# The merged projection's row blocks: the next block's turn moved between two output halves, and a buffer moved between two state tags

## The chip, the cores and the metric

The kernel runs on one core of one Trainium2 chip. The metric is the device time of one execution in microseconds (us). The notation of the profile is: PE is TensorE (PEld its weight loads), DVE is VectorE, ACT is ScalarE, POOL is GpSimd, SP is the engine that issues most of the transfers. L1227 is line 1227 of the kernel.

## The reference, cut to what matters

One layer of a diffusion backbone works on 9 blocks of 128 rows: block 0 is the prompt (128 tokens), blocks 1 to 8 are the 1024 latent tokens. Attention heads and four bidirectional mLSTM heads stand side by side and are merged by one output projection, which a SwiGLU feed-forward layer follows.

```python
attn_o = attention(aq, keys, vals)
hm, st_f, st_b = mlstm_bidir(heads(mq), heads(mk) * (MLSTM_DK ** -0.5), heads(mv), gates, init_f, init_b)
hm = rmsnorm(hm.transpose(0, 2, 1, 3), mlstm_norm_w.reshape(MLSTM_HEADS, MLSTM_DV))
hm = (hm.reshape(B, T, MLSTM_WIDTH) * jax.nn.sigmoid(mo.astype(F32))).astype(x.dtype)
mix = jnp.concatenate([attn_o, hm], axis=-1) @ w_out
x = x + g1 * mix
h2 = rmsnorm(x, norm2_w) * (1 + sc2) + sh2
x = x + g2 * swiglu(h2, w_gu, w_down)
```

The mLSTM scan carries a matrix state of 128x128 and a vector of 128 for each head and direction. The latent tokens' scans start from states that are given as inputs, `state_C` and `state_n`.

## The kernel before, in words

A product in fp32 is made of three matmuls: each operand is split into a high part (a cast on ACT) and the rest (a subtraction, mostly on DVE), and the products high·high, high·low and low·high are added in PSUM. So a weight piece needs a transfer, a cast (L157, `whi`) and a subtraction (L137, `wlo`), and a block of rows needs to be turned by PE (L116, four transposes of 128x128), cast on ACT and subtracted on DVE before it can be multiplied.

The program has three long stretches.

*The mLSTM heads.* For head h, `head_project` makes q, k, v and gate products of all 9 blocks and adds each block to the states: the forward state at once (L824, DVE), while the backward contributions are put aside by ACT (L828, tag `cs`). `head_mlstm` then runs the backward chain over blocks 8 to 2 (L862, DVE, seven steps) and the scan over blocks 0 to 8; it is woven with the projection of the next head and with the first third of the attention. Each head loads two initial states (L807 and L808 on SP's queue): `c0f` for the forward scan, `c0b` for the backward one. The backward one is read by the first step of L862 and for the last time by the matmul L898 at block 8, the last block of the scan. `c0f` has two buffers, `c0b` one; the running states have `CSB` = 21 buffers of the tag `cs`, and each head takes 16 of them.

*The prefill* (`prefill`, L1188). It computes the mLSTM half of the merged projection for all 9 blocks. `load_hm` brings a block's normalised mLSTM rows from DRAM (tag `hmr`, two buffers), `mix(b)` turns them (L116) into one PSUM bank, casts them (L1227, ACT) and subtracts (L137, DVE) into a tile of the tag `mx` (three buffers, one of which holds the prompt's gate `gx_all` at first). `half(b, n)` multiplies them with one of two halves of the output columns: 12 matmuls (L1183 to L1185) into one bank, then DVE multiplies by the gate (L1144, or L1243 for blocks 6 to 8) and POOL adds it to the row (L1145 or L1244). The pool of such banks has four. `end(b)` makes the sum of squares for blocks 0 to 2 (L1345, ACT, which needs POOL's additions of both halves), and after blocks 2, 3 and 4 the second norm of rows 0, 1 and 2 (`norm2`: L1361, eight transposes, L1371, L1376). After every yield of the prefill 0.35 of a step of the second third of the attention is woven in (S at L1075, maximum L1077, exponential L1078, L1081, L1082, transposing transfers L1084 and L1085, values L1099 and L1100), and each of its PE steps is held behind the last output matmul written so far.

*The feed-forward stretch*, for three groups of three blocks: `gate_up` (L1382 to L1384) and `down` (L1155 to L1157), with the rest of the attention woven in.

What sets the order: a planner goes through the program with a model of each instruction's time and, on each engine, takes the ready instruction with the highest priority. Priority is the order in which the code is written, except that a `hot(n)` block counts as written n instructions earlier. The order that comes out is fixed; on the chip each engine works it off in turn, and an instruction that waits holds all behind it on its engine. Buffers are given out of a pool for each tag, and an instruction that needs one waits until one is released.

Of the kernel before, what the change touches and what calls it, by code (L numbers as in the profile page):

```python
# [8 lines left out]
F32 = mybir.dt.float32  # L9
# [10 lines left out]
P = 128  # L20
D = 1024
KD = D // P
NB = 9
# [14 lines left out]
LAST = [(0, 5), (5, 5), (10, 4), (14, 4), (18, 4)]  # L38
PAIRS = [(0, 1), (2, 3), (4,), (5, 6), (7, 8)]
NG = 4  # L40
CSB = 21
SINGLES = [(b,) for b in range(NB)]


# [1 line left out]
def hybrid_step(ctx: ExitStack, tc: tile.TileContext, I: dict, O: dict):  # L46
# [8 lines left out]
    def hot(n):  # L55
        return tc.high_priority(n)

    def nm(s):
        uid[0] += 1
        return f"{s}_{uid[0]}"  # L60
# [19 lines left out]
    def xrow(b):  # L80
        if b == 0:
            return I["x_prompt"][0]
        return I["x_sample"][0, (b - 1) * P : b * P, :]
# [20 lines left out]
    def bank():  # L104
        return psum["mm"].tile([P, 512], F32, name=nm("mm"), tag="mm")
# [9 lines left out]
    def transpose(out, in_, n=P):  # L115
        nc.tensor.transpose(out, in_, ident[:n, :n])  # L116
# [19 lines left out]
    def sub(out, full, hi, eng):  # L136
        (dve if eng == "dve" else pool).tensor_tensor(out=out, in0=full, in1=hi, op=ALU.subtract)  # L137
# [410 lines left out]
    mlp = es1.enter_context(tc.tile_pool(name="mlp", bufs=1, reuse_waits="tile"))  # L548
    mwh = mlp.tile([P, 512], F32, name="mwh")
    for tag, shape, bufs, dt in (("hm", [P, NB, P], 2, F32), ("ssh", [P, NB], 2, F32), ("nu", [P, 2, P + 1], 4, F32), ("it", [P, 2, P + 1], 3, F32),  # L550
                                 ("dn", [P, 2], 3, F32), ("jkh", [P, P], 1, BF16), ("sd", [P, 2, P], 4, F32), ("dt", [P, 2, P], 4, F32),
                                 ("so", [P, P], 9, F32), ("va", [P, P + 1], 9, F32), ("kT", [P, P], 9, F32), ("th", [P, P], 1, F32),
                                 ("kt", [P, P], 2, F32), ("wv", [P, 2, P + 1], 2, F32), ("c0f", [P, P + 1], 2, F32), ("c0b", [P, P + 1], 1, F32),
                                 ("cs", [P, P + 1], CSB, F32), ("qTm", [P, CT], 2 * NCH, F32)):
        mlp.tile(shape, dt, name=f"lay_{tag}", tag=tag, bufs=bufs)

# [2 lines left out]
    def gate_work(mlp):  # L559
        def g1(name, dt=F32, rows=P):  # L560
            return mlp.tile([P, P + 1], dt, name=name, tag="cs", bufs=CSB)[0:rows, 0:P]

# [211 lines left out]
    def head_project(h, st):  # L774
# [28 lines left out]
        st["s"] = states = {}  # L803
        st["raw"] = raws = {}
        for d in range(2):
            c0 = mlp.tile([P, P + 1], F32, name=nm("c0"), tag=("c0f", "c0b")[d], bufs=2 - d)
            dma(c0[:, 0:P], I["state_C"][0, 0, d, h])  # L807
            dma(c0[:, P : P + 1], I["state_n"][0, 0, d, h].rearrange("(p o) -> p o", o=1))  # L808
            states[d, 1 if d == 0 else NBL] = c0

        def update(b, kt, va):
# [6 lines left out]
            for d in range(2):  # L818
                if b == (NBL if d == 0 else 1):
                    continue  # L820
                add = pc[:, d * (P + 1) : (d + 1) * (P + 1)]
                cn = mlp.tile([P, P + 1], F32, name=nm("cs"), tag="cs", bufs=CSB)
                if d == 0 and b > 0:
# [314 lines left out]
    def t2():  # L1138
        return ft.tile([P, 512], F32, name=nm("t2"), tag="t2", bufs=3)

    def add_gated(x1, ps, g, n, eng=dve):
        cs = slice(n * 512, (n + 1) * 512)
        t = t2()
        dve.tensor_tensor(out=t, in0=ps, in1=g, op=ALU.mult)  # L1144
        eng.tensor_tensor(out=x1[:, cs], in0=x1[:, cs], in1=t, op=ALU.add)  # L1145
# [17 lines left out]
    def out_pieces(half, n):  # L1163
        pieces = []
        for j in range(2):
            r0 = half * 512 + 2 * j * P
            rows = w_out[r0 : r0 + 2 * P, n * 512 : (n + 1) * 512].rearrange("(a p) n -> p a n", p=P)
            pieces.append(load_piece([(full_view, rows)], (2, 512)))
        return pieces

    def out_gates():
        gs = []
        for n in range(2):
            gl = xg.tile([P, 512], F32, name=nm("gl"), tag=("gl", "gx")[n], bufs=1)
            dma(gl, g_d[0, 1:2, n * 512 : (n + 1) * 512].to_broadcast([P, 512]))
            gs.append(gl)
        return gs

    def out_block(ws, n, th, tl):
        ps = bank()  # L1180
        for k in range(4):
            wh, wl = ws[n][k // 2]
            mm(ps, th[:, k], wh[:, k % 2, :], start=(k == 0), stop=False)  # L1183
            mm(ps, th[:, k], wl[:, k % 2, :], start=False, stop=False)  # L1184
            loaded["pe"] = mm(ps, tl[:, k], wh[:, k % 2, :], start=False, stop=(k == 3)).ins  # L1185
        return ps

    def prefill(cur, nxt):  # L1188

        x1s = cur["x1"], nxt["x1"]  # L1190
        cur["rs"] = []

        def load_hm(b):
            if b >= NB:
                return None
            hm = xe.tile([P, 512], F32, name=nm("hmr"), tag="hmr", bufs=2)
            if b < CB:
                loaded["hm"] = dma(hm, hm_d[0][b * P : (b + 1) * P, :]).ins
            else:
                r = dma(hm.rearrange("p (h n) -> p h n", n=P), hm_d[b // CB][:, :, b % CB * P : (b % CB + 1) * P])  # L1200
                if b == CB:
                    loaded["hm"] = r.ins
            return hm

        def load_x1(b):
            if CB <= b < 2 * CB:
                dma(x1s[1][b % CB], xrow(b))

        hms = [load_hm(0), load_hm(1)]
        ws = [out_pieces(1, 0)]  # L1210
        gs = out_gates()
        gx_all = xe.tile([P, D], F32, name="gx_all", tag="mx", bufs=3)
        gate = loaded["gate"] = dma(gx_all, g_d[0, 0:1, :].to_broadcast([P, D])).ins
        ws.append(out_pieces(1, 1))
        cur["gate"] = loaded["piece"]
        gx = [gx_all[:, n * 512 : (n + 1) * 512] for n in range(2)]
        mixed = {}

        def mix(b):
            t = xe.tile([P, NQ, P], F32R, name=nm("mx"), tag="mx", bufs=3)  # L1220
            th, tl = mixed[b] = t[:, 0:4], t[:, 4:8]
            hm = hms.pop(0)
            ps = bank()
            for j in range(4):
                transpose(ps[:, j * P : (j + 1) * P], hm[:, j * P : (j + 1) * P])
            psv = ps.rearrange("p (j x) -> p j x", j=4)
            nc.scalar.copy(th, psv)  # L1227
            sub(tl, psv, th.bitcast(F32), "dve")
            with tc.issue_after(gate):
                hms.append(load_hm(b + 2))  # L1230

        def half(b, n):
            c, i = divmod(b, CB)
            cs = slice(n * 512, (n + 1) * 512)
            ps = out_block(ws, n, *mixed[b])
            g = gx[n] if b == 0 else gs[n]
            if c < 2:
                add_gated(x1s[c][i], ps, g, n, pool)
            else:
                xt = t2()  # L1240
                dma(xt, xrow(b)[:, cs])
                t = t2()
                dve.tensor_tensor(out=t, in0=ps, in1=g, op=ALU.mult)  # L1243
                pool.tensor_tensor(out=xt, in0=xt, in1=t, op=ALU.add)  # L1244
                dma(x1_d[i][:, cs], xt)

        def end(b):
            if b < CB:
                with hot(200):
                    cur["rs"] += stats(x1s[0][b : b + 1])  # L1250
            if 2 <= b < CB + 2:
                yield from norm2(0, cur, b - 2)

        for b in range(2):
            mix(b)
            yield
        for b in range(2):
            half(b, 0)
            yield
        for b in range(2):  # L1260
            load_x1(b + 2)
            half(b, 1)
            yield
            yield from end(b)
        for b in range(2, NB):
            load_x1(b + 2)
            mix(b)
            yield
            for n in range(2):
                half(b, n)  # L1270
                yield
            yield from end(b)

    def attn_out_first(oT, ready):
# [66 lines left out]
    def stats(rows):  # L1341
        s1 = fp.tile([P, CB], F32, name=nm("s1"), tag="s1", bufs=3)
        for i, x in enumerate(rows):
            jk = ft.tile([P, D], BF16, name=nm("jk"), tag="t2", bufs=3)
            act(jk, x, AF.Square, accum_out=s1[:, i : i + 1])  # L1345
        r = rsqrt(fp, s1[:, 0 : len(rows)], len(rows), 1.0 / D, CB)
        return [r[:, i : i + 1] for i in range(len(rows))]
# [174 lines left out]
    for _ in prefill(cur, nxt):  # L1522
        due += 0.35
        while due >= 1.0:
            with tc.issue_after(cur["gate"]), tc.issue_after(loaded["gate"]), tc.issue_after(loaded["hm"]), tc.issue_after(loaded["pe"]):
                next(att, None)
            due -= 1.0
# [100 lines left out]
```

## Time and profile before

| | us |
|---|---|
| median of three runs | 1536.48 (1536.39 to 1541.33) |
| the profiled execution | 1540.57 |
| its span, first to last instruction | 1538.8 |
| PE busy in the span | 1479.7 |
| DVE, ACT, POOL busy | 1019.1, 771.3, 272.3 |

The prefill's first transposes start at 489.59 us, its last output matmul starts at 576.8 us, and the feed-forward stretch fills the rest. In the views, a row of the timeline gives the start, the duration, the engine, the line, the operation, its tiles and, in brackets, how long the engine stood idle before it and what ended that. A row of stretches gives for each engine the busy time and the number of instructions, then the granted clock of TensorE, the busy share of the transfer engines and their rate. A matmul's duration in the trace includes its way through the array, so that the distance between the starts of two matmuls tells more than their durations.

### The profile page before, as it was taken

Reading aid. Unit: us, or ns where it says so; the run is one execution under the profiler, and the core shown is the slowest. Engines: PE = TensorE matmul, PEld = TensorE weight load, DVE = VectorE, ACT = ScalarE, POOL = GpSimd, SP = SyncE. Lnnn points to the kernel's source line nnn. Section 1 sums busy time; section 2 is a strip of 40 time slices with the busy share of each in tenths; the row PEclk is TensorE's granted clock in tenths of the full one; section 3 lists DMA queues with packets and bytes.
Section 4 is the critical chain, followed back from the end, with each engine's and each line's share of the span. In section 5 each row is a group of like instructions: output and inputs, shape, how many; then the busy total and the mean of one; then the engine's idle time right before and its main releaser. Section 6 shows DMA issues by size and latency. Waiting matters only on the chain.

```text
span 1538.8 us, 23409 instructions
## 1 busy us (share of the span) xinstructions
PE 1479.7 (96%) x8539; PEld 1245.3 (81%) x8539; DVE 1019.1 (66%) x2025; ACT 771.3 (50%) x1429; POOL 272.3 (18%) x354
## 2 busy tenths in 40 slices
PE   6799999999989899999999999999999999999997
PEld 3545567677766679899898989989898989999996
DVE  4878654838657875878646497887856584554554
ACT  4764475847654544555332445556553443333333
POOL 0112423233434441010010101000010101101110
PEclk9799999999999999999999999999999999999998
DMA  9664323523365566978634457877754445544441
GB/s 359 191 203 148 100 71 42 119 52 66 75 212 167 156 145 193 214 152 199 170 123 149 152 154 239 188 175 175 181 135 143 145 155 160 157 131 137 141 142 60
DMA packets 387113, 233.77 MB, mean 152 GB/s; under 512 B 170102, under 2 KB 347462, under 8 KB 386998
## 3 DMA queue, kind: packets, MB, share of 16 engines
q1 hardware_dynamic: 385006, 228.69, 54.0%
q10 hardware_dynamic: 1864, 3.20, 1.1%
q8 instruction: 67, 1.10, 0.3%
q14 instruction: 48, 0.39, 0.1%
q0 software_dynamic: 128, 0.39, 0.1%
HBM read 182.21 MB, written 11.69 MB: 126 GB/s over the span
## 4 chain that ended last, share of the span: by engine, by line
PE 58%; DVE 3%; DMA 1%; ACT 1%; issue 0%; ACTq 0%
PE mm L1383 12%; PE mm L1384 12%; PE mm L1382 12%; PE mm L1155 5%; PE mm L1156 5%; PE mm L1157 5%; PE S L1075 3%; PE po L1099 1%; PE po L1100 1%; PE mm L1185 1%; PE mm L1184 1%; PE mm L1183 1%; DVE fl L1371 1%; DVE wlo L137 1%; DVE t L1144 0%; DVE x L1145 0%
## 5 line engine op out<-in xcount | busy, mean ns | idle before, releaser
L157 ACT CAST whi<-raw 128x1024 fp32r<-128x1024 f32 (+1 forms) x216 | 221.8, 1027 | 390.3 <-PE mm L1383 151.5
L137 DVE TENSOR_TENSOR wlo<-raw,whi 128x1024 fp32r<-128x1024 f32 (+1 forms) x216 | 260.4, 1205 | 183.4 <-ACT whi L157 182.8
L1383 PE MATMUL mm<-aTl,whi 128*128 128x384 f32 x1056 | 355.9, 337 | 2.7 <-DVE aTl L137 2.7
L1384 PE MATMUL mm<-aTh,wlo 128*128 128x384 f32 x1056 | 354.1, 335 | 0.0
L1382 PE MATMUL mm<-aTh,whi 128*128 128x384 f32 x1056 | 352.5, 335 | 0.0
L137 POOL TENSOR_TENSOR hl<-tn,hl 128x384 fp32r<-128x384 f32 x66 | 85.3, 1292 | 848.7 <-ACT hl L1405 713.8
L1383 PEld LDWEIGHTS mm<-aTl,whi 128*128 128x128 f32 x1056 | 198.4, 188 | 3.9 <-DVE aTl L137 3.3
L1384 PEld LDWEIGHTS mm<-aTh,wlo 128*128 128x128 f32 x1056 | 198.4, 188 | 0.1
L1382 PEld LDWEIGHTS mm<-aTh,whi 128*128 128x128 f32 x1056 | 198.0, 188 | 0.6
L1156 PE MATMUL mm<-wlo,hl 128*128 128x512 f32 x372 | 145.3, 391 | 0.0
L1155 PE MATMUL mm<-whi,hl 128*128 128x512 f32 x372 | 144.1, 392 | 0.0
L1157 PE MATMUL mm<-whi,hl 128*128 128x512 f32 x372 | 142.6, 392 | 0.0
L1082 DVE SCALAR_TENSOR_TENSOR pl<-pr,st,ph 128x1152 f16<-128x1152 f32 (+1 forms) x72 | 96.0, 1334 | 33.0 <-ACT ph L1081 32.9
L1078 ACT ACTIVATE pr<-S,st 128x1152 f32<-128x1152 f32 (+1 forms) x72 | 81.2, 1128 | 34.5 <-DVE st L1077 33.9
L1077 DVE TENSOR_REDUCE st<-S 128x1 f32<-128x1152 f32 (+1 forms) x72 | 88.9, 1235 | 13.6 <-PE S L1075 12.9
L1081 ACT ACTIVATE ph<-pr,st 128x1152 f16<-128x1152 f32 (+1 forms) x72 | 83.8, 1164 | 20.9 <-DVE st L1080 8.0
L506 PE MATMUL wi<-headw,hT 128*128 128x384 f16 x288 | 93.9, 326 | 0.2 <-ACT th L792 0.2
L508 PE MATMUL wi<-headw,hT 128*128 128x384 f16 x288 | 93.9, 326 | 0.0
L507 PE MATMUL wi<-headw,hT 128*128 128x384 f16 x288 | 93.9, 326 | 0.0
L1144 DVE TENSOR_TENSOR t<-mm,gl 128x512 f32<-128x512 f32 x102 | 68.8, 685 | 27.5 <-DMA gl<-g_d 12.2
L1075 PE MATMUL S<-kst,qT 128*128 128x384 f32 (+1 forms) x400 | 84.4, 344 | 2.4 <-ACT pr L1078 2.4
L1157 PEld LDWEIGHTS mm<-whi,hl 128*128 128x128 f32 x372 | 69.9, 188 | 14.4
(396 smaller groups left out, 2647.7 us busy)
## 6 DMA issues: line engine op xcount, KB each, us to landing
raw<-in_w_gu_dram SPq DMA_DIRECT2D x132, 512.0 KB
raw<-in_w_down_dram SPq DMA_DIRECT2D x60, 512.0 KB
a<-in_w_ada_dram SPq DMA_DIRECT2D x24, 512.0 KB
gl<-g_d SPq DMA_DIRECT2D x36, 256.0 KB
aw<-in_w_ada_dram SPq DMA_DIRECT2D x16, 512.0 KB
iraw<-in_w_in_dram SPq DMA_DIRECT2D x32, 256.0 KB
raw<-in_w_out_dram SPq DMA_DIRECT2D x12, 512.0 KB
x<-in_x_sample_dram SPq DMA_DIRECT2D x11, 512.0 KB
```

Source lines behind the costliest of these rows:

```text
L137: (dve if eng == "dve" else pool).tensor_tensor(out=out, in0=full, in1=hi, op=ALU.subtract)
L157: nc.scalar.copy(hi[:, :n], raw[:, :n])
L506: mm(ps[:, :n], ah, wh[:, k % 2, c0 : c0 + n], start=(k == 0), stop=False)
L507: mm(ps[:, :n], ah, wl[:, k % 2, c0 : c0 + n], start=False, stop=False)
L1075: mm(S[:, n, 0:w], qT[:, h, :], kst[kv][:, t, c0 + n * w : c0 + (n + 1) * w], start=(t == 0), stop=(t == 1))
L1082: dve.scalar_tensor_tensor(out=plv, in0=prv, scalar=st[:, 3:4], in1=phv, op0=ALU.mult, op1=ALU.subtract)
L1155: mm(ps, ah, wh[:, k % 2, :], start=(k == 0), stop=False)
L1156: mm(ps, ah, wl[:, k % 2, :], start=False, stop=False)
L1157: mm(ps, al, wh[:, k % 2, :], start=False, stop=(k == nk - 1))
L1382: mm(ps, wh[:, k, :], th[:, k, :], start=(k == 0), stop=False)
L1383: mm(ps, wh[:, k, :], tl[:, k, :], start=False, stop=False)
L1384: mm(ps, wl[:, k, :], th[:, k, :], start=False, stop=(k == KD - 1))
```

## The change

In the prefill, `mix(b + 1)` now stands between `half(b, 0)` and `half(b, 1)` for blocks 2 to 7, `mix(2)` stands between `half(0, 1)` and `half(1, 1)`, and the loop no longer begins a block with its own `mix`. `end(0)` comes before `mix(2)`. No instruction is added or removed there. The tag `c0b` gets a second buffer, and the tag `cs` loses one of its 21; a buffer of either has the same size.

```diff
-CSB = 21
+CSB = 20
...
-                                 ("kt", [P, P], 2, F32), ("wv", [P, 2, P + 1], 2, F32), ("c0f", [P, P + 1], 2, F32), ("c0b", [P, P + 1], 1, F32),
+                                 ("kt", [P, P], 2, F32), ("wv", [P, 2, P + 1], 2, F32), ("c0f", [P, P + 1], 2, F32), ("c0b", [P, P + 1], 2, F32),
...
-            c0 = mlp.tile([P, P + 1], F32, name=nm("c0"), tag=("c0f", "c0b")[d], bufs=2 - d)
+            c0 = mlp.tile([P, P + 1], F32, name=nm("c0"), tag=("c0f", "c0b")[d], bufs=2)
...
-        for b in range(2):
-            load_x1(b + 2)
-            half(b, 1)
-            yield
-            yield from end(b)
+        load_x1(2)
+        half(0, 1)
+        yield
+        yield from end(0)
+        load_x1(3)
+        mix(2)
+        yield
+        half(1, 1)
+        yield
+        yield from end(1)
         for b in range(2, NB):
             load_x1(b + 2)
-            mix(b)
-            yield
-            for n in range(2):
-                half(b, n)
+            half(b, 0)
+            yield
+            if b + 1 < NB:
+                mix(b + 1)
                 yield
+            half(b, 1)
+            yield
             yield from end(b)
```

More of the change, by code (lines that the diff above doesn't have):

```diff
@@ L1259, in prefill @@
             yield
-        for b in range(2):
-            load_x1(b + 2)
+        load_x1(2)
[8 more added lines that the diff above has]
+        yield from end(1)
+        for b in range(2, NB):
+            load_x1(b + 2)
+            half(b, 0)
[3 more added lines that the diff above has]
+                yield
             half(b, 1)
             yield
-            yield from end(b)
-        for b in range(2, NB):
-            load_x1(b + 2)
-            mix(b)
-            yield
-            for n in range(2):
-                half(b, n)
-                yield
             yield from end(b)
```

## The prediction

> **What bounds the kernel now.** First the page's busy shares and its forty slices, for the engine that is full and where it is not; then stretches of 25 us around the prefill.
>
> ```profile
> PE 1479.7 (96%) x8539; PEld 1245.3 (81%) x8539; DVE 1019.1 (66%) x2025; ACT 771.3 (50%) x1429; POOL 272.3 (18%) x354
> PE   6799999999989899999999999999999999999997
> PEclk9799999999999999999999999999999999999998
> ...
> 475.00:500.00 25.00, 22.14 (x119) 16.27 (x118) 18.80 (x68) 12.49 (x37) 11.75 (x14) 0.93 0.56 180
> 500.00:525.00 25.00, 21.00 (x88) 15.94 (x87) 21.97 (x60) 15.75 (x25) 9.85 (x6) 0.90 0.65 196
> 525.00:550.00 25.00, 22.46 (x121) 18.76 (x120) 20.00 (x35) 13.41 (x23) 15.31 (x10) 0.96 0.48 102
> 550.00:575.00 25.00, 24.32 (x133) 19.98 (x133) 15.65 (x25) 10.61 (x13) 8.83 (x6) 1.00 0.65 160
> 600.00:1525.00 925.00, 922.32 (x5043) 855.65 (x5042) 609.78 (x870) 411.84 (x542) 84.25 (x65) 1.00 0.59 158
> ```
>
> PE is the bound: from 600 to 1525 us it stands idle for 925 − 922.3 = 2.7 us at full clock, so that stretch gives nothing and only moves forward or back as a whole. The prefill, 489 to 577, is where PE has holes and where the granted clock falls below 1. Who makes the holes is in the waits of PE from 485 to 600.
>
> ```profile
> PE mm L1183 <- ACT mx L1227: 4.8, 4, 2.3
> PE S L1075 <- ACT pr L1078: 1.6, 1, 1.6
> PE mm L1185 <- DVE mx L137: 1.2, 2, 0.9
> PE mm L1185 <- DVE rv L127: 0.3, 1, 0.3
> ```
>
> The output matmuls wait for the cast of the block's own rows (L1227), and then for its subtraction (L137). The fourth row is the same subtraction, in block 2, put down to another DVE instruction that ended last. The change aims at these rows. One of the four casts is block 0's, which the change leaves where it is; the worst is block 3's:
>
> ```profile
> 491.81 0.49 PE L1183 MATMUL mm<-whi,mx 128*128 128x512 f32 x1 [1.13 <-ACT mx L1227]
> ...
> 517.07 0.60 PE L116 MATMUL mm<-ident,hmr 128*128 128x128 f32 x4
> 519.99 0.77 PE L1183 MATMUL mm<-whi,mx 128*128 128x512 f32 x1 [2.32 <-ACT mx L1227]
> 521.50 0.80 PE L1185 MATMUL mm<-whi,mx 128*128 128x512 f32 x1 [0.32 <-DVE mx L137]
> 526.79 0.44 PE L1185 MATMUL mm<-whi,mx 128*128 128x512 f32 x1
> ...
> 512.20 0.39 PE L1183 MATMUL mm<-whi,mx 128*128 128x512 f32 x1
> 512.43 0.39 PE L1184 MATMUL mm<-wlo,mx 128*128 128x512 f32 x1
> ...
> 518.32 1.06 ACT L1345 ACTIVATE jk<-x1a 128x1024 bf16<-128x1024 f32 x1 [3.57 <-POOL x1a L1145]
> 519.37 0.56 ACT L1227 CAST mx<-mm 128x512 fp32r<-128x512 f32 x1
> ...
> 516.00:520.00 4.00, 1.68 (x16) 1.41 (x14) 3.90 (x8) 1.69 (x4) 1.58 (x2) 1.00 0.61 132
> 520.00:524.00 4.00, 3.68 (x8) 2.48 (x9) 3.79 (x21) 4.00 (x7) 0.00 (x0) 0.51 0.08 24
> 524.00:528.00 4.00, 4.00 (x14) 3.12 (x13) 2.10 (x5) 1.23 (x3) 0.98 (x1) 0.64 0.39 74
> ```
>
> Block 3's rows are turned by 517.67, but ACT stands at L1345, block 2's sum of squares, which waits 3.57 us for POOL; the cast is behind it, and PE, with nothing else left, behind the cast. Then the granted clock is 0.51 for four microseconds and 0.64 for the next. The 14 steps between matmul starts from 519.99 to 526.79 take 6.80 us; at the step of the undisturbed rows, 0.23, they would take 3.2. Of the 3.6 lost, 0.32 is the wait for the subtraction, and 3.3 the clock.
>
> **The change part by part.** *The moved turns, what goes.* `mix(2)` to `mix(8)` move: each has four transposes on PE, one cast, one subtraction and the issue of one `hmr` load on SP. None is added. The waits that should end: casts 4.8 − 1.13 (block 0) = 3.7 us; subtractions 1.2 + 0.3 = 1.5; and the clock behind block 3's hole, 3.3, since the rows of 516 to 528 show the fall directly behind the only stretch in which PE did 1.68 of 4 us. That is 8.5 us gross.
>
> *What covers a moved turn.* The path from transposes to subtraction is block 2's:
>
> ```profile
> 507.67 0.60 PE L116 MATMUL mm<-ident,hmr 128*128 128x128 f32 x4
> 508.31 0.58 ACT L1227 CAST mx<-mm 128x512 fp32r<-128x512 f32 x1 [1.77 <-PE mm L116]
> 509.74 0.68 DVE L137 TENSOR_TENSOR mx<-mm,mx 128x512 fp32r<-128x512 f32 x1
> ```
>
> It ends at 510.42, 2.75 us after the first transpose, and PE itself is engaged for about 0.4 of it (eight transposes take 1.03 us in a row below, four 0.60). The cover is `half(b, 1)`: 12 steps of 0.23, 2.8 us, plus whatever attention stands behind it. So the cover is just enough when ACT and DVE come at once. In block 3 the same path took 521.50 − 517.07 = 4.4 us with ACT held up, 1.6 more than the cover; under the change the cast is written ahead of the sum of squares that held it. The new remainder lies between 0 and 1.6 for each of the three blocks that are beside the second norm (4.8); as DVE is busy 21.97 of 25 us there, I take 0.5 each, 1.5 in all.
>
> *Banks.* The turn's bank is now held beside both halves' banks, and the norm takes two of the four as well:
>
> ```profile
> 514.92 0.39 PE L1185 MATMUL mm<-whi,mx 128*128 128x512 f32 x1
> 516.20 1.03 PE L116 MATMUL mm<-ident,y 128*128 128x128 f32 x8
> 516.26 0.68 DVE L1144 TENSOR_TENSOR t<-mm,gl 128x512 f32<-128x512 f32 x1
> 523.24 1.04 DVE L1371 TENSOR_SCALAR fl<-mm,scale,shift 128x128 f32<-128x128 f32 x3
> ```
>
> The norm's eight transposes at 516.20 fill two banks that DVE empties only at 523.24 + 1.04. In that time one half, one turn and the next half have to share two, and a half's bank comes free 516.26 + 0.68 − 514.92 − 0.39 = 1.6 us after its last matmul. So PE may newly wait up to 1.6 us before `half(b, 1)`, less the 0.4 of transposes, in three blocks: 0 to 3.6; I take 1.5, since DVE's queue was the slow part in the rows above too.
>
> *Queues.* On SP each `hmr` load moves forward with its turn; it waits for its buffer, so the transposing transfers of the attention queue behind it. The buffer comes free with the transposes, which PE does without waiting, and block 4's load, after block 2's turn, has the whole of block 3 to land: nothing. POOL gets no instruction earlier or later but by its inputs. On ACT, a cast that waits for an `mx` tile would hold the sums of squares; for block 2 that tile is block 0's, free with the last matmul of `half(0, 1)`, just before: nothing. The wait of S for the exponential (1.6) belongs to the attention and stays; its end is a gain of 1.6.
>
> *The second `c0b`.* Now the last head's load can be issued only after the scan before has read the buffer:
>
> ```profile
> 446.60 0.26 ACT L828 COPY cs<-mm 128x129 f32<-128x129 f32 x1
> 441.58 0.56 SPq L808 DMA_DIRECT2D c<-in_state_n_dram  x1
> 447.86 1.24 DVE L131 TENSOR_TENSOR rt<-ry 128x9 f32<-128x9 f32 x1
> 449.30 0.35 DVE L862 SCALAR_TENSOR_TENSOR cs<-c,decb,cs 128x129 f32<-128x129 f32 x1 [0.20 <-DMA c<-in_state_n_dram]
> 450.04 0.49 PE L875 MATMUL mm<-qT,kT 128*128 128x128 f32 x2 [2.42 <-DVE sd L883]
> 448.00:456.00 8.00, 5.11 (x36) 3.56 (x37) 7.80 (x22) 2.68 (x8) 3.04 (x2) 0.79 0.49 159
> ```
>
> The load takes from 441.58 to 449.3 to land, while the last block's contribution is there at 446.86. But DVE is busy until 449.10 with other work, so the wait itself is 0.20 us. The best case is that the planner, with the state early, draws the chain forward and PE's hole of 8 − 5.11 = 2.9 us and the clock loss of the same row (0.21 × 8 = 1.7) go: 4.6. The worst is that the seven steps of 0.35, 2.4 us, come ahead of the `sd` (L883) that PE waits for. I take a gain of 0.5, by the row of the wait itself.
>
> *One `cs` fewer.* In the third head:
>
> ```profile
> L828 ACT COPY cs<-mm x9: 267/269/318, 322.7 to 376.3; 128x129 f32<-128x129 f32 x9
> L898 PE MATMUL mm<-cs,qT x28: 273/275/276, 309.6 to 366.7; 128*128 128x129 f32 x28
> ```
>
> The scan of the head before has read its states by 366.7, while this head's contributions come in until 376.3. Halfway, at 350, this head holds about 8 of its 16, and the scan, 40 of 57 us through, keeps about 5: 13 of 20. So it costs nothing; were the scan three blocks later, one wait of about a scan's block, 57/7 = 8 us, could appear.
>
> *The sum*: −8.5 + 1.5 + 1.5 − 0.5 = −6.0 us. The profiled execution (1540.57, of which 1538.8 span) is 4.1 above the median; a difference carries over, so from 1536.48 comes **1530.5 us**. Behind the prefill nothing gives it back, because PE is full there.
>
> On the clock, the rows above show a fall after a hole of 2.32 us. The Trainium skill, "TensorE: Matmul & The Clock Gate", Part 1, says that the clock halves after at least one idle window of about 3.4 us. The trace agrees in the factor (0.51) and differs in the length, as PE was idle no 3.4 us on end. By that rule the fall would not be the hole's, the 3.3 would stay, and the time would be 1533.8.
>
> **The rivals.** *A, slower: banks.* The place is `half(b, 1)` in blocks 3, 4 and 5, where two banks are with the norm. If PE's new wait there grows past about 2 us, the clock falls again, and one such wait costs what block 3's costs now: 2.3 + 0.3 + 3.3 = 5.9. Three cost 17.7, against 8.5 saved: 1545.7. It decides from two such waits on. For it: DVE's 88% from 500 to 525. Against it: a half's bank lag of 1.6 less 0.4 is under 2.
>
> *B, it does nothing.* The planner ranks by written order but starts what is ready; if it keeps ACT at the sum of squares ahead of the cast, or the attention's S ahead of the half, the waits only change place: 1536.5, within 2. Against it: the cast is now written one half ahead of that sum.
>
> *C, the clock falls anyway.* A similar hole, 2.42 before 450.04, stands in the row with clock 0.79; the hole of 1.6 before S is followed by nothing like it, as the clock of 525 to 550 is 0.96, and what lacks there is the tail of block 3's fall. If it isn't the hole's length that decides, a window of PE's lesser work elsewhere in the prefill gets the low clock: 1530.5 + 3.3 = 1533.8.
>
> *D, more.* No remainder, no bank waits, the wait of S gone, and the start of the last scan drawn forward: −8.5 − 1.6 − 4.6 = −14.7, 1521.8.
>
> **How the numbers follow.** Forecast (1527 to 1534): 0.38. A: 0.16, B: 0.18, C: 0.13, D: 0.15. 0.5% of the median is 7.7 us, about what a measurement of this kernel tells from no change. Faster than 1528.8: D and a quarter of the forecast's chance, 0.25. Slower than 1544.2: most of A, 0.13. Same: 0.62. The range reaches from near D's end to where A has one and a half of its waits: 1523 to 1541.
>
> **What would show it.** The row of L1183 waiting for L1227 should shrink to block 0's, in about 1.1 us; no L1227 should stand behind an L1345 that waits for POOL; the clock from 500 to 550 should be 1 but for the start at 491.81; the transposes of block b + 1 should stand between two halves on PE; the last prefill matmul should come some 6 us earlier. L807 for the last head's `c0b` should be issued long before 441, with no wait of L862 for it. The prediction is wrong if PE waits for L1144 or L1243 to free a bank, if the clock falls in blocks 3 to 5, or if the heads' stretch ends more than 3 us from where it does.

## The result, and the profile after

| | before | after |
|---|---|---|
| median of 13 runs of each, us | 1540.67 | 1535.38 |
| the profiled execution, us | 1540.57 | 1535.49 |
| its span, us | 1538.8 | 1533.7 |

The ratio is 0.9972, with a 95% interval of 0.9964 to 0.9980: 4.3 us less (3.1 to 5.5; the two medians lie 5.3 apart), where the forecast had 6.0. That is a real gain and a small one, within the 0.5% that the forecast had called no change. The 1530.5 itself lies 4.9 below the median, and 4.2 of that is the base: the three runs of the kernel before that were shown have a median of 1536.48, and the 13 runs here 1540.67. Two executions of kernels in the experiments took 5172.03 and 1663.96 us, and the medians and ratios given there are those of the others.

The first view is the waits of PE from 485 to 600 us in the changed kernel (engine, operation and line, what it waited for, then us in total, times, longest). Below L1257 a line of the changed kernel has a number higher by 7: L1352 is the old L1345, L1368 the old L1361, L1389 the old L1382.

```profile
PE S L1075 <- ACT pr L1078: 3.1, 1, 3.1
PE mm L1184 <- DVE wlo L137: 1.9, 4, 0.6
PE mm L1185 <- DVE mx L137: 1.7, 1, 1.7
PE mm L1183 <- ACT mx L1227: 1.1, 1, 1.1
...
PE mm L1183 <- DVE st L1080: 0.5, 1, 0.5
...
PE mm L1183 <- DVE mx L137: 0.3, 1, 0.3
```

The wait for the cast has shrunk from 4.8 to block 0's 1.1, as forecast. The wait of S for the exponential, which the prediction left at 1.6, is now 3.1 and the largest. The last two rows are waits of a half for a bank, 0.8 us in all; how that is seen stands with the account of the prediction. Next the same stretches as before the change, and four of 4 us around block 3 (length, busy time of each engine, then the granted clock):

```profile
475.00:500.00 25.00, 20.85 (x101) 15.10 (x101) 18.40 (x61) 12.49 (x32) 10.62 (x13) 1.00 0.62 202
500.00:525.00 25.00, 19.64 (x89) 16.14 (x89) 21.67 (x52) 14.11 (x22) 8.84 (x6) 0.93 0.70 192
525.00:550.00 25.00, 24.11 (x133) 20.09 (x132) 21.66 (x44) 14.82 (x26) 14.73 (x11) 1.00 0.42 91
550.00:575.00 25.00, 25.00 (x137) 20.54 (x137) 16.56 (x26) 10.62 (x15) 7.72 (x6) 1.00 0.77 193
...
512.00:516.00 4.00, 2.98 (x15) 2.33 (x13) 4.00 (x12) 1.04 (x3) 2.47 (x1) 1.00 0.75 148
516.00:520.00 4.00, 1.67 (x8) 1.35 (x9) 3.90 (x16) 2.44 (x4) 1.28 (x1) 0.97 0.09 18
520.00:524.00 4.00, 4.00 (x16) 3.48 (x15) 3.76 (x7) 4.00 (x8) 0.00 (x0) 0.61 0.38 72
524.00:528.00 4.00, 4.00 (x21) 3.26 (x20) 3.27 (x10) 4.00 (x7) 1.91 (x2) 1.00 0.61 137
```

From 525 on the prefill is nearly full (24.11 and 25.00 of 25, against 22.46 and 24.32). At block 3 PE is not: it does 1.67 of 4 us, almost the 1.68 of before, and the clock falls behind it. The hole has not gone; other instructions stand around it. The timeline of PE, with one row of DVE and one of ACT:

```profile
513.54 1.21 PE L1075 MATMUL S<-kst,qT 128*128 128x384 f32 x6
514.59 0.40 PE L1185 MATMUL mm<-whi,mx 128*128 128x512 f32 x1
518.12 1.32 PE L1075 MATMUL S<-kst,qT 128*128 128x384 f32 x6 [3.14 <-ACT pr L1078]
...
521.22 0.78 PE L1183 MATMUL mm<-whi,mx 128*128 128x512 f32 x1
...
515.38 1.35 DVE L1077 TENSOR_REDUCE st<-S 128x1 f32<-128x1152 f32 x1
...
516.76 1.22 ACT L1078 ACTIVATE pr<-S,st 128x1152 f32<-128x1152 f32 x1 [3.72 <-DVE st L1077]
```

Between two S of the attention stands one matmul of block 2's second half. S has a single buffer, so the second waits until the exponential of the first has read it: S, maximum on DVE (held 0.6 us by the small steps of a reciprocal root), exponential on ACT, 4.6 us in all. The first half of block 3, whose rows are ready, stands behind the second S and the norm's transposes and begins at 521.22, at half clock.

Two numbers carry the comparisons that follow. The prefill is counted from the first turn to the first gate matmul of the feed-forward stretch, and that stretch from its first gate matmul to the start of its last. In the changed kernel:

```profile
L116 PE MATMUL mm<-ident,hmr x36: 270/272/328, 487.2 to 560.9; 128*128 128x128 f32 x36
...
L1389 PE MATMUL mm<-aTh,whi x1056: 331/334/423, 572.3 to 1505.9; 128*128 128x384 f32 x176
```

So the prefill takes 85.1 us and the stretch 933.6. For all kernels that were profiled, with the granted clock from 508 to 532 us, where block 3 lies:

| kernel (executions) | prefill, us | feed-forward, us | clock 508 to 532 |
|---|---|---|---|
| before (3) | 87.4, 87.2, 87.0 | 934.0, 933.1, 934.3 | 0.86, 0.86, 0.93 |
| buffers alone | 87.4 | 933.1 | 0.93 |
| after (2) | 85.1, 84.6 | 933.6, 933.2 | 0.93, 0.93 |
| turns alone | 83.5 | 934.8 | 0.93 |
| before, attention one step later | 87.9 | 938.1 | 0.93 |
| after, attention one step later | 82.4 | 937.0 | 1.00 |
| after, held up to block 3 (2) | 82.1, 82.9 | 933.3, 934.2 | 1.00, 1.00 |
| after, held to the last steps | 81.5 | 935.1 | 1.00 |

A clock of 0.93 over 24 us is a loss of 0.07 × 24 = 1.7 us, and 0.86 one of 3.4. The clock column leaves out block 0. There the clock of 488 to 498 is 0.83, a loss of 1.7 us, in two of the three executions of before, in one of the two of after and in one of the two held up to block 3, and 1.00 in the others of these. So two prefills of this table can differ by 1.7 us for no reason of an edit.

### The profile page after: what moved, and what is told of

Same layout as the page of the kernel before. It is cut to its first block, busy times and chain, and to the rows that moved or that the text cites. A ratio compares the mean times of both kernels' runs of the same rounds, so it can differ in the third digit from the quotient of the medians.

```text
span 1533.7 us, 23404 instructions
## 1 busy us (share of the span) xinstructions
PE 1475.5 (96%) x8539; PEld 1242.4 (81%) x8539; DVE 1019.8 (66%) x2025; ACT 772.3 (50%) x1429; POOL 266.7 (17%) x354
## 4 chain that ended last, share of the span: by engine, by line
PE 61%; DVE 3%; ACT 1%; issue 0%; DVEq 0%
PE mm L1390 12%; PE mm L1391 12%; PE mm L1389 12%; PE mm L1155 5%; PE mm L1156 5%; PE mm L1157 5%; PE S L1075 3%; PE po L1099 2%; PE po L1100 2%; PE mm L1183 1%; PE mm L1185 1%; PE mm L1184 1%; DVE fl L1378 1%; DVE wlo L137 1%; DVE t L1144 0%; DVE x L1145 0%
## 5 line engine op out<-in xcount | busy, mean ns | idle before, releaser
L137 DVE TENSOR_TENSOR wlo<-raw,whi 128x1024 fp32r<-128x1024 f32 (+1 forms) x216 | 260.4, 1206 | 182.4 <-ACT whi L157 180.8
L1389 PE MATMUL mm<-aTh,whi 128*128 128x384 f32 x1056 | 353.1, 335 | 0.0
L137 POOL TENSOR_TENSOR hl<-tn,hl 128x384 fp32r<-128x384 f32 x66 | 83.8, 1270 | 847.4 <-ACT hl L1412 755.5
L1389 PEld LDWEIGHTS mm<-aTh,whi 128*128 128x128 f32 x1056 | 198.1, 188 | 0.5
L1144 DVE TENSOR_TENSOR t<-mm,gl 128x512 f32<-128x512 f32 x102 | 68.7, 684 | 24.7 <-DMA gl<-g_d 9.3
```

Of the source, the lines that this page charges most:

```text
L1389: mm(ps, wh[:, k, :], th[:, k, :], start=(k == 0), stop=False)
```

## The experiments

**The turns alone.** The changed kernel with the buffers of before.

```diff
-CSB = 20
+CSB = 21
...
-("c0b", [P, P + 1], 2, F32)
+("c0b", [P, P + 1], 1, F32)
...
-tag=("c0f", "c0b")[d], bufs=2)
+tag=("c0f", "c0b")[d], bufs=2 - d)
```

> Edit: the moved turns alone; cs keeps 21 buffers and c0b one. Theory T (the whole gain is the moved turns): ratio to the kernel before 0.997, the same as with the whole change, and the prefill (first turn to first feed-forward matmul) takes about 85 us against 87.4. Rival R1 (the earlier load of the initial state carries part: the first 450 us were 3 us shorter in the changed kernel's profile): ratio 0.9985 to 1.0. Rival R2 (the lost cs buffer costs something that the whole change hides): ratio under 0.996.

Measured: 1534.88 us, ratio 0.9969 (0.9957 to 0.9980), the whole of the change's gain, as theory T has it. In its waits of PE stand the same two rows, the cast's at block 0's size and that of S:

```profile
PE S L1075 <- ACT pr L1078: 3.1, 1, 3.1
...
PE mm L1183 <- ACT mx L1227: 1.1, 1, 1.1
```

**The buffers alone.** The kernel before with the second `c0b` and one `cs` fewer (the lines above, the other way round).

> Edit: the kernel before with cs at 20 and c0b at two buffers, turns not moved. T: ratio 1.000, within 0.0005, since PE, DVE, ACT and POOL keep their order through the heads and the chain's wait for the load was 0.20 us; the prefill has its 2.3 us hole before block 3 and the clock falls there. R1: ratio 0.998 to 0.9985. R2: over 1.0005.

Measured: 1540.13 us, ratio 0.9999 (0.9989 to 1.0010). The buffers are worth nothing that can be measured. What they do is in the changed kernel's DVE timeline: the first step of the last backward chain no longer waits for its state, but PE's wait behind the chain stays (the last row is from the waits of PE from 430 to 600, where it was 2.4).

```profile
446.12 0.34 DVE L862 SCALAR_TENSOR_TENSOR cs<-c,decb,cs 128x129 f32<-128x129 f32 x1
...
451.13 2.09 DVE L862 SCALAR_TENSOR_TENSOR cs<-cs,decb,cs 128x129 f32<-128x129 f32 x1
...
PE mm L875 <- DVE sd L883: 2.1, 1, 2.1
```

From first to last step the chain takes 5.0 us, as before (449.30 in the prediction's row to 454.33). The load was never what it waited for, but for 0.2 us.

**The attention one step later, in both kernels.** If the hole at block 3 is the S that now stands too early, holding all attention phases of the prefill back by one step should take it out.

```diff
-    due = 0.0
+    due = -0.35
     for _ in prefill(cur, nxt):
         due += 0.35
```

> Edit: the changed kernel, with the attention woven into the prefill one yield later (its count starts at -0.35). So the scores of each attention head are written behind a half that is ready, where the changed kernel has them ahead of block 3's first half. Theory T2 (the changed kernel still has block 3's hole in front of a scores matmul that waits 3.1 us for the exponential, and the clock falls behind it for 3.4 us): that wait goes, PE waits in the prefill fall from about 10 us to about 5, a further 3 to 5 us are gained, ratio 0.994 to 0.995. Rival R3 (the attention is the true chain of the prefill, so the wait only changes place, or comes back in the feed-forward stretch where more of the attention is left): ratio 0.997 as before the edit.

> Edit: the kernel before, turns not moved, with the attention one yield later as in e3. T2 with T (the two are separate: the turn's path of 2.75 us stays open in front of every block): casts still hold PE for 3 to 4 us in all, ratio 0.998 to 1.0. Rival R4 (the attention's place is all that matters, and the moved turns are worth nothing of their own): the ratio of e3.

Measured: the changed kernel held back 1537.74, ratio 0.9984 (0.9974 to 0.9993); the kernel before held back 1543.99, ratio 1.0022 (1.0013 to 1.0031). The turns are worth as much in this position of the attention as in the other (0.9984 against 1.0022), but holding back costs both kernels something, and the expected gain on top did not come. Yet the hole did go: S waits 0.6 us instead of 3.1, the clock stays at 1 and the prefill is 2.7 us shorter. The feed-forward stretch is 3.4 us longer, which is the second form of rival R3: theory T2 is right about the hole and wrong about the time. The rows of that stretch, from the timelines of PE, ACT and SP and from the stretches:

```profile
584.81 0.37 PE L1099 MATMUL po<-phT,vs 128*128 128x256 f16 x1 [2.73 <-DMA phT<-ph]
...
577.25 1.22 ACT L1078 ACTIVATE pr<-S,st 128x1152 f32<-128x1152 f32 x1
...
580.32 1.98 SPq L1084 DMA_TRANSPOSE phT<-ph  x1
...
580.00:592.00 12.00, 9.27 (x53) 8.44 (x53) 6.37 (x7) 5.65 (x8) 1.00 (x1) 0.86 0.81 186
```

The first value product of the feed-forward waits 2.73 us for a transposing transfer, and the clock falls behind it: 2.7 + 0.14 × 12 = 4.4 us lost. The chain behind that transfer begins with the last S of the prefill, which ran a step later; its exponential came at 577.25. In the changed kernel that exponential is at 571.57, and nothing waits. In the kernel before, held back, the same product waits 2.4 us, and the waits for the cast grow to 7.5 us, where 3 to 4 were expected, because an S has moved on that stood between turn and half in block 5, for example, and covered the cast:

```profile
PE mm L1183 <- ACT mx L1227: 7.5, 6, 2.3
PE po L1099 <- DMA phT<-ph: 2.4, 1, 2.4
```

**Held back only up to block 3, or to the last steps.** Two kernels keep the later S at block 3 and catch up afterwards, one right behind it and one six steps further on.

```diff
-    due = 0.0
-    for _ in prefill(cur, nxt):
-        due += 0.35
+    due = -0.35
+    for step, _ in enumerate(prefill(cur, nxt)):
+        due += 0.7 if step == 14 else 0.35
```

> The changed kernel with the attention's phases of the prefill held back by one step up to block 3 and caught up right behind it, so that from block 4 on the order is that of the changed kernel. Theory T3 (holding back the attention is worth something at block 3, and what the held-back kernel lost it lost to one transpose by DMA at the first value product of the feed-forward): the wait of S for the exponential shrinks from 3.1 us to under 1, the clock stays at 1 from 508 to 540, and no value product waits for phT behind 575 us. Gain against the changed kernel about 2.5 (wait) + 1.6 (0.13 of 12 us of clock) = 4 us, ratio to the kernel before 0.9945 (0.993 to 0.996). Rival R4 (the value product waits for its transposes again, though the last S stands where the changed kernel has it): as the held-back kernel, 0.998. Rival R5 (the hole at block 3 is filled with an attention phase that was free elsewhere, so that another hole opens by block 6): as the changed kernel, 0.997.

The other has `step == 20`.

> As the kernel that holds back by one step all through, but the attention catches up at the last step but a few, so that only the last S of the prefill stands again where the changed kernel has it (between the two halves of the last block). Theory T3: what decides is how early that last S is issued before the first value product of the feed-forward; the 2.7 us wait for phT and the half clock behind it go, and the time is that of e5, ratio 0.9945 (0.993 to 0.996). Rival R4 (the wait comes from the traffic of the transfers at the start of the feed-forward, or from all phases being late): it stays above 1.5 us and the ratio is 0.997 to 0.999.

Measured: held up to block 3, 1532.22, ratio 0.9955 (0.9942 to 0.9968); held to the last steps, 1534.97, ratio 0.9970 (0.9959 to 0.9980). The first does at block 3 what theory T3 says, and its ratio lies in the range given, but the gain over the changed kernel is about 2.6 us by the ratios and not 4. Its rows at block 3, from the timeline of PE and the stretches:

```profile
512.82 1.22 PE L1075 MATMUL S<-kst,qT 128*128 128x384 f32 x6
...
515.84 0.48 PE L1183 MATMUL mm<-whi,mx 128*128 128x512 f32 x1
...
519.88 1.32 PE L1075 MATMUL S<-kst,qT 128*128 128x384 f32 x6 [0.61 <-ACT pr L1078]
...
508.00:532.00 24.00, 21.15 (x111) 17.04 (x110) 22.89 (x62) 15.25 (x25) 9.96 (x8) 1.00 0.51 127
```

The first half of block 3 now begins at 515.84 and lies between the two S. Of the time up to the next S, 7.1 us instead of 4.6, PE waits 0.61. A part of what is missing is rival R5: another hole has opened at block 5, where the second half waits for one of the norm's two banks (`fl` is what DVE makes of them). The kernel's waits for banks from block 4 on add up to 2.4 us (1.06 and 1.29), against 0.8 and 1.1 in the two executions of the changed kernel.

```profile
542.53 0.47 PE L1183 MATMUL mm<-whi,mx 128*128 128x512 f32 x1 [1.29 <-DVE fl L1378]
```

In the other kernel theory T3 fell: its ratio lies outside the range of T3 and at the edge of rival R4's. The last S stands where the changed kernel has it, and the clock holds, but the first value product still waits:

```profile
579.13 0.27 PE L1099 MATMUL po<-phT,vs 128*128 128x256 f16 x1 [1.09 <-DMA phT<-ph]
...
581.19 0.27 PE L1100 MATMUL po<-plT,vs 128*128 128x256 f16 x1 [0.73 <-DMA plT<-pl]
```

That is 1.8 of the 2.7 us, with no fall of the clock in this execution, and its span, 1530.9, is that of the other kernel (1531.1). Why the medians still differ by 2.7 us the two profiles do not tell.

**The kernels before and after again, and the held one beside them.** The profiles of before and after differ by 3.1 us before the change can act: the first scaling of q (L846) starts at 165.2 and at 162.1, with the same instructions in the same order on PE, DVE, ACT and POOL until then. Two more profiles of the kernel before were to show whether that is chance, and the changed and the held kernel were timed on one chip.

> The kernel before, unchanged, profiled again. In its first profile the clock stood at 0.83 from 60 to 80 us and the first qT scaling (L846) came at 165.2 us; in the changed kernel's at 1.00 and 162.1, with the same instructions in the same order until then. Theory P (the fall at 70 to 76 us comes by chance of an execution, and the 3 us are none of the change's): the profiles of the kernel before differ among themselves, L846 between 162 and 165.5, so that one of these two lies within 1 us of the changed kernel's 162.1. Rival K (something of the change decides it, for example where the second buffer puts the tiles): both again 0.83 and 165 within 0.5.

> The kernel before once more, for the same question. Theory P: L846 somewhere between 162 and 165.5, not the same as in the other two to 0.5 us. Rival K: 165 again, clock 0.83 from 60 to 80 us.

> The changed kernel, unchanged, on the same chip as the kernel that holds the attention back up to block 3. Ratio to the kernel before 0.997 (0.996 to 0.998) by all theories. Prefill from the first turn to the first matmul of the feed-forward 85 us within 1. For the first 80 us: theory P, L846 anywhere from 162 to 165.5; rival K, 162 within 0.5 and a clock of 1.00.

> The kernel that holds the attention back by one step up to block 3, on the same chip as the changed kernel. If holding back is a gain of its own, its ratio lies below the changed kernel's by 0.0017 (0.0008 to 0.0026), 0.9955; if its first result was chance, both lie at 0.997 within 0.0005. Prefill 82 us within 1, S waiting for the exponential under 1 us.

It is chance, as theory P has it, though one of the starts, 161.0, lies a little below the range that it gave. The rows of 60 to 80 us and of L846, first of the profile that the prediction had, then of the third profile of the same kernel:

```profile
60.00:80.00 20.00, 17.21 (x135) 10.99 (x132) 16.29 (x67) 11.92 (x28) 4.70 (x6) 0.83 0.34 108
...
L846 DVE TENSOR_SCALAR qT<-wi,isc x12: 602/611/618, 165.2 to 385.5; 128x384 f32<-128x384 f32 x12
```

```profile
60.00:80.00 20.00, 15.55 (x149) 9.54 (x146) 19.08 (x79) 14.48 (x31) 3.78 (x6) 1.00 0.46 150
...
L846 DVE TENSOR_SCALAR qT<-wi,isc x12: 602/610/618, 161.0 to 381.3; 128x384 f32<-128x384 f32 x12
```

The second profile has 162.3, the changed kernel's second 163.4. So of the 5.1 us between the first two profiles, 3.1 belong to no edit.

The changed kernel came out at 1535.58, ratio 0.9970 (0.9959 to 0.9982), and the held one at 1533.31, ratio 0.9956 (0.9943 to 0.9969), the same two ratios as the first time. Each interval overlaps the other a little, but both times the held kernel's ratio is the lower one, by 0.17% and 0.14%, about 2.4 us. It is the fastest version here, 0.44% under the kernel before.

## Why the prediction was right or wrong

**The bound and the place: right.** PE is the bound, and only the prefill pays. Over the executions of the table the prefill went from 87.2 us (mean of before's three) to 84.8 (mean of the changed kernel's two; the turns alone, 83.5). The feed-forward stretch, 933.1 to 934.8 in all of these and with the buffers alone, gave nothing back.

**The casts, 3.7 us: right.** The row went from 4.8 to 1.1 (1.7 in the second profile), and no wait for a cast is left behind block 0.

**The subtractions, 1.5 us: not found.** Rows of L1185 waiting for `mx` or `rv` and of L1184 waiting for `wlo` made up 2.1 us in the profile that the prediction read, and 3.6 in the changed kernel's. In block 2 the cast ran early, but its subtraction stood on DVE behind a weight's subtraction and a maximum:

```profile
504.74 0.59 ACT L1227 CAST mx<-mm 128x512 fp32r<-128x512 f32 x1
...
504.75 1.97 DVE L137 TENSOR_TENSOR wlo<-raw,whi 128x1024 fp32r<-128x1024 f32 x1 [1.79 <-ACT whi L157]
506.64 1.34 DVE L1077 TENSOR_REDUCE st<-S 128x1 f32<-128x1152 f32 x1
507.91 0.67 DVE L137 TENSOR_TENSOR mx<-mm,mx 128x512 fp32r<-128x512 f32 x1
...
508.64 0.50 PE L1185 MATMUL mm<-whi,mx 128*128 128x512 f32 x1 [1.71 <-DVE mx L137]
```

The prediction had seen that DVE was 88% busy there and booked a remainder of 1.5 for it; in its own sum the gain and the remainder cancel, and here too nothing is left of them. These waits differ by about 2 us between executions of one kernel, so nothing finer can be said.

**Bank waits, 1.5 us: right in kind, 0.8 to 1.1 in size.** No row names a bank, but the first output matmul of a half (L1183) reads only what ACT has cast, the rows and the weight's high part, and writes into a bank. So where it waits for DVE, DVE has a bank to empty first. In the changed kernel this happens twice, in block 4. The first half waits 0.31 us (0.56 in the second profile) until L137 has read the bank of that block's turn. The second half waits 0.47 us (0.49) until L1144 has read the first half's bank, at 535.77 + 0.67 = 536.44; the `st` that the view names is only the last DVE instruction to end:

```profile
535.77 0.67 DVE L1144 TENSOR_TENSOR t<-mm,gl 128x512 f32<-128x512 f32 x1
536.36 0.14 DVE L1080 TENSOR_SCALAR st<-st 128x1 f32<-128x1 f32 x1
536.42 2.00 DVE L1378 TENSOR_SCALAR fl<-mm,scale,shift 128x128 f32<-128x128 f32 x6
...
536.49 0.50 PE L1183 MATMUL mm<-whi,mx 128*128 128x512 f32 x1 [0.47 <-DVE st L1080]
```

The norm's two banks are emptied only from 536.42 on, so the halves and the turn share the other two, as the prediction says. The profiles of before have no wait of L1183 for DVE. With the turns alone the two waits make 1.4 us. Rival A needed waits of over 2 us and a fall of the clock behind each: the longest in any of these kernels is 1.30, and the clock of 538 to 548, around it, is 1.00.

**"The wait of S for the exponential (1.6) belongs to the attention and stays": this is the step that failed.** In the kernel before that wait stood ahead of block 4's first half:

```profile
533.28 1.32 PE L1075 MATMUL S<-kst,qT 128*128 128x384 f32 x6 [1.64 <-ACT pr L1078]
```

In the changed kernel it is gone, and a new one of 3.1 us stands ahead of block 3. The attention is drawn by steps of the prefill, so moving the turns between the halves moved the steps under the attention's phases too, and two S came to stand with one matmul between them, ahead of the half that could have filled the gap. Rival B named this (the attention's S ahead of the half), but as an all-or-nothing case. Of the three signs of being wrong that the prediction gave, two came: PE waits for L1144 to free a bank, and the clock falls in block 3. The prediction asked for each moved instruction what it passes, and not what is woven by count beside it.

**The clock, 3.3 us: the mechanism right, the size not, since it hung on the same step.** With the S hole in the place of the cast hole the clock fell again, by 1.7 us in each profile of the changed kernel and of the turns alone. In the three profiles of the kernel before it had cost 3.4, 3.4 and 1.7, and 1.7 with the buffers alone, so the gain is about 0.9 on the mean. The prediction had the 3.3 from one execution. That the fall is the hole's, and not a thing of its own as rival C had it, the held kernels show: where PE has no hole over 1.2 us from 508 to 532, the clock of that stretch is 1.00 in all four profiles. That makes 1.2 us no threshold: at block 0 the clock fell behind waits of 1.13 and 1.09 us in two executions of the kernel before and did not behind 1.09 in the third.

On this the Trainium skill, "TensorE: Matmul & The Clock Gate", Part 1, says that activity is watched in free-running windows of about 3.4 us. The trace agrees with the size: half clock for one or two such windows loses 1.7 or 3.4 us, and the kernel before shows either. It agrees with the chance, too, as one order of instructions gave both. It does not show a window idle from end to end: the longest hole of block 3 is 3.15 us, and the one of 3.14 lies in a stretch where PE did 1.67 of 4 us. How much work keeps a window busy no run here shows.

**The buffers, 0.5 us: nothing.** 0.9999, by the row of the wait itself 0.2 us. That one `cs` fewer costs nothing was right.

**The sum.** Casts 3.7 and clock 0.9 gained, S 1.5 and the bank waits 0.8 lost, subtractions about even: 2.3 us, against 2.4 by the prefill's means. The spans of the same five profiles differ by 3.2 us on the mean; the other 0.8 lies half ahead of the prefill and half in the feed-forward stretch, less than executions of one kernel differ by there (the prefill starts between 486.6 and 489.6 in those of the kernel before). The timed runs give 4.3 (3.1 to 5.5), and what they have beyond the profiles is located in no stage. That the measured gain lies as near to 6.0 as it does is in part luck, as the terms that were found add up to 2.3. Without the new wait of S the gain is of the size of the forecast: the kernel held up to block 3 gains 0.45% (0.32 to 0.58), 6.9 us. It is not quite the forecast's own case, as its S waits 0.6 where the prediction left 1.6.

## What to carry to other kernels

Where side work is woven in by counted steps, moving an item of the main work moves the side work as well: before pricing the move, list the new neighbours of every side phase on the bound engine, above all two that share a single buffer. A hole that is closed in one place should be looked for again within a few microseconds, and the test is to shift the side work alone and bring it back, since a shift kept up to the end is paid at the next join. A view of waits names what ended last; what the waiting instruction reads and writes tells what it waited for. And a difference of a few microseconds between two profiles is no finding until one kernel has been profiled twice.

## What the runs showed of the hardware

The early part of the program took up to 4.2 us more or less in three profiles of one kernel (L846 from 161.0 to 165.2), with the granted clock of 60 to 80 us at 0.83, 0.91 and 1.00. A fall of the clock came in steps of 1.7 us, so that behind one hole of 2.3 us the kernel before lost 1.7 us in one execution and 3.4 in two. At block 0 one order of instructions gave a fall behind a wait of 1.09 us in one execution and none behind the same wait in another. And a wait of 2.73 us at the value product took the clock down (0.86 over 12 us), while two of 1.09 and 0.73 within 2 us did not, in one execution each.
